# Four edits to the order of TensorE's work in a hybrid recurrent layer: the triangular inversion's two updates, half-block gemms, SSD's carried part, the output weights' splits

## The chip, the cores and the metric

One Trainium2 chip, one core, one launch. The metric is the device time of one execution in microseconds; lower is better. Engines are called as in the profile: PE is TensorE's matmuls, PEld its weight loads, DVE is VectorE, ACT is ScalarE, POOL is GpSimd, SP is the queue that issues the DMAs.

## The reference, cut to what matters

The layer takes 1024 prompt tokens and 8 x 8 sample tokens (1088 tokens of width 1024). It projects them, runs four recurrent mixers of width 256, and projects back:

```
z   = x @ w_in
A   = RG-LRU(conv(z_a)) * SiLU gate
B   = gated RMSNorm(SSD(conv(z_b)))          chunked scan
C   = RMSNorm(GatedDeltaNet(conv(z_c))) * SiLU gate
D   = GLU(S5(z_d)) * SiLU gate
out = concat(A, B, C, D) @ w_out
x   = LayerNorm(alpha * x + out)
```

Gated DeltaNet (GDN), per chunk and head, needs the inverse of a unit lower triangular matrix:

```
m     = where(strict, beta * (k k^T) * gamma, 0)
tmat  = inverse(eye + m)
value = tmat @ (beta * v);  kcum = tmat @ (beta * exp(decay) * k)
w     = value - kcum @ s
o     = qdec @ s + (q k^T * gamma) @ w
s     = chunk_decay * s + kdec^T @ w
```

SSD, per chunk and head:

```
y  = (C B^T * L * dt) @ x  +  (C * exp(acum)) @ h_prev  +  d * x
h  = chunk_decay * h + (exp(acum_last - acum) * dt * B)^T @ x
```

## The kernel before, in words

**Gemms.** Tokens are held transposed in SBUF as a rounded part and a rest (`xh`, `xl`), and so are the weights. A product of 128 output columns is `gemm_ch` (L237): it loads and splits the weights (`load_w`, L142: a DMA, an ACT copy into `wh`, a DVE subtraction into `wl`) and calls `gemm_block` (L227) for three blocks of tokens of 320, 384 and 384 columns. A block is 24 matmuls into one PSUM bank (lines L232, L233, L234), and then ACT or DVE takes the bank away. Twelve of these 18 products run in the part of the program that the change touches.

**Two streams.** From about 200 us on, the last line of the program, `run(merge((gdn(...), 130.0), (side(), 280.0)))`, walks two generators. Each `yield c` says how much work was issued since the last one, and `merge` (L112) goes on with the stream that is furthest behind its share. This sets the order in which instructions are emitted. The framework then orders each engine's instructions from it when the program is built, earlier emitted ones first where they are expected to be ready; an engine runs its list strictly in that fixed order. So between two matmuls of the inversion there stand a few matmuls of a gemm block that was emitted as a whole.

**The GDN stream** takes nine chunks (64 sample tokens, then 8 x 128 prompt tokens). While `tail` of a chunk runs (state update, output), `make` of the next one runs `prep` and `invert` (L834). `invert` doubles the size of the inverted blocks level by level, 3 levels for the sample chunk and 6 for each other, 51 in all. X and Y (the inverse and its transpose, four heads side by side) are kept in one PSUM bank `XY`, X in the first 256 columns and Y in the others. A level is:

- L861: T = A X on PE, into another bank; L863: DVE multiplies it by the level's mask into `t_`; L852 (`spread`): two DVE copies into `tb`
- L868: X += Y^T T on PE (reads `t_` and the copy `yb` of Y); L870: ACT copies X out
- L873: Y += T^T Y on PE (reads `tb` and Y); L876: two ACT copies into `yb`; L878: ACT copies Y out

A `yield 0.2` stands after X and another after Y. After the levels comes one correction step (E by L882 and L883, its DVE part L885 into `tb`, then L890 on PE).

**The side stream** (L1347) issues the gemms, RG-LRU, SSD (`chunk`, L1067) and then the out projection (`project`, L1395). SSD uses a pool of two PSUM banks (tag "b") in turn for `xt`, `gam`, `cb0`, `cb1`, `yd`, `yo0`, `yo1`, `st` and `yT`. C B^T is L1090; DVE makes M of it (L1093); M x is L1101 into the bank `yd`; the carried part C h is L1114 into the banks `yo0` and `yo1`; L1117 adds it.

**The out projection.** `woh` and `wol`, the split parts of w_out, take the SBUF space of `xh` and `xl`, so that no split can be written before the last gemm has read those. `w_half` (L1400) loads eight pieces of 128 x 512, one for each k; ACT writes `woh` (L1405), DVE `wol` (L1406). The loads go into the buffers of the gemms' weights (tags `wr` with 2 buffers, `wh` and `wl` with 4 each). Then for each of nine token chunks: load x (L138), gate v (L1422), split the eight pieces of the mixers' output for k = 0 to 3 and 4 to 7 (ACT L1428, DVE L1429, also in buffers of the tags `wh` and `wl`), and for each half of the columns 24 matmuls (L1439 to L1441), a residual add and statistics; the second half of w_out is split between the first chunk's own splits and its matmuls. Layer norm and the store follow.

Of the kernel before, what the change touches and what calls it, by code (L numbers as in the profile page):

```python
# [14 lines left out]
OP = mybir.AluOpType  # L15
# [4 lines left out]
P = 128  # L20
# [32 lines left out]
def hybrid_step(ctx, tc, I, O, dbg=None):  # L53
    nc = tc.nc
    mm = nc.tensor.matmul
# [171 lines left out]
    def gemm_block(w, a, b, evac):  # L227
        whi, wlo = w
        ps = gemm_bank()
        o = ps[:, :b - a]  # L230
        for k in range(8):
            mm(o, whi[k], xh[:, k, a:b], start=(k == 0), stop=False)  # L232
            mm(o, whi[k], xl[:, k, a:b], start=False, stop=False)  # L233
            mm(o, wlo[k], xh[:, k, a:b], start=False, stop=(k == 7))  # L234
        evac(a, b, o)

    def gemm_ch(c0, evac):  # L237
        w = load_w(w_tile(c0), P)
        for a, b in BLOCKS:
            gemm_block(w, a, b, evac)  # L240
            yield 3.7
# [525 lines left out]
    def gdn(wk, up, q, k, v, rk, rq):  # L767
# [66 lines left out]
        def invert(d):  # L834
# [23 lines left out]
            for l in range(3 if n == NS else 6):  # L858
# [8 lines left out]
                for h in range(4):  # L867
                    mm(pX[:n, h], idh[:n, :n] if Y is None else yb[:n, h, :n], t_[:n, h], start=False, stop=False, skip_group_check=True)  # L868
                X = pk(f16("X", "X", 256, 2))
                act(X[:n], pX[:n], AF.Copy)  # L870
                yield 0.2
                for h in range(4):
                    mm(pY[:n, h], tb[:n, h, :n], idp[:n] if Y is None else Y[:n, h], start=False, stop=h == 3, skip_group_check=True)  # L873
# [175 lines left out]
    def ssd(wk, up, x, BT, CT):  # L1049
# [17 lines left out]
        def chunk(ti):  # L1067
# [20 lines left out]
            for g in range(2):  # L1088
                sl = slice(g * 64, g * 64 + 64)
                mm(pcb[g][:n, :n], BT[sl, c], CT[sl, c], start=True, stop=True)  # L1090
            M = g2("M")
# [7 lines left out]
            py = bank("yd")  # L1099
# [5 lines left out]
            tt(y[:n], py[:n, :256], y[:n], OP.add)  # L1105
            if ti != 1:
# [3 lines left out]
                else:  # L1110
                    pyo = [bank("yo0"), bank("yo1")]
                    for g in range(2):
                        sl = slice(g * 64, g * 64 + 64)
                        mm(pyo[g][:, :P], CT[sl, c], Hs[sl].rearrange("p h d -> p (h d)"), start=True, stop=True)  # L1114
                    yof = lambda h: pyo[h // 2][:, 64 * (h % 2):64 + 64 * (h % 2)]
# [279 lines left out]
    def project():  # L1395
# [4 lines left out]
        def w_half(e):  # L1400
            for k_ in range(8):
# [6 lines left out]
        w_half(slice(0, 512))  # L1408
# [5 lines left out]
        for i in range(9):  # L1414
# [9 lines left out]
            for k0 in (0, 4):  # L1424
                h_, l_ = (wp.tile([P, 536], F32R, name=nm(t), tag=t)[:, :4 * n].rearrange("p (k n) -> p k n", k=4) for t in ("wh", "wl"))
# [121 lines left out]
```

## Time and profile before

| | |
|---|---|
| median of 3 runs | 619.89 us (618.18 to 621.85) |
| the profiled execution, its own time | 620.72 us |
| its span, first to last instruction | 619.0 us |
| granted TensorE clock, mean over the span | 0.988 |
| instructions | 11787 |
| DMA | 44.14 MB, mean 71 GB/s |

Times in the rows are microseconds from the start of the span. In a timeline row stand the start, the duration, engine, line, operation, the tiles written and read, the shape and how many equal instructions were merged; in brackets the idle time of the engine before it and what ended it. Matmuls are pipelined, and their ends are modelled: the distance from one start to the next is what a matmul takes of PE.

### The profile page before, as it was taken

What the parts mean: (1) busy time and instruction counts of PE and PEld (TensorE: products, weight loads), DVE (VectorE), ACT (ScalarE), POOL (GpSimd) and SP (SyncE); (2) the same over time, 40 slices, a digit from 0 to 9 for tenths busy, and PEclk for the clock granted to TensorE, in tenths of its full rate; (3) what the DMA queues carried; (4) which work ended last, traced back from release to release, by engine and by line L of the source; (5) the groups of instructions that cost most, each with busy time, mean ns of one, the idle gap of its engine ahead of it and who ended that gap; (6) DMA issues with size and microseconds to landing.
All of it is one profiled execution on the core that took longest, in us unless ns stands there. A gap on an engine that the chain in (4) does not pass through costs nothing.

```text
span 619.0 us, 11787 instructions
## 1 busy us (share of the span) xinstructions
PE 586.3 (95%) x4284; PEld 503.4 (81%) x4284; DVE 464.9 (75%) x1372; ACT 325.0 (53%) x877; POOL 62.7 (10%) x165
## 2 busy tenths in 40 slices
PE   5999899999999999999999999999999799999995
PEld 5999899999998776888887888787877557778883
DVE  6997989943768586699888867786775789866655
ACT  5545255345364457897665665766546657332210
POOL 8220100000100000211001000110010000110000
PEclk9999999999899999999999999999999999999998
DMA  8552212041310010010142100110033221121221
GB/s 301 171 169 63 77 65 78 16 131 73 119 40 19 19 44 29 17 35 19 39 143 80 43 5 23 37 43 10 2 125 110 77 94 53 40 101 69 102 103 68
DMA packets 24187, 44.14 MB, mean 71 GB/s; under 512 B 3201, under 2 KB 10433, under 8 KB 24129
## 3 DMA queue, kind: packets, MB, share of 16 engines
q1 hardware_dynamic: 24128, 43.38, 21.4%
q8 instruction: 34, 0.56, 0.4%
q14 instruction: 25, 0.20, 0.1%
HBM read 32.97 MB, written 10.41 MB: 70 GB/s over the span
## 4 chain that ended last, share of the span: by engine, by line
PE 65%; DVE 16%; ACT 8%; issue 6%; DMA 3%; POOL 2%; SPq 1%; DVEq 0%; ACTq 0%; POOLq 0%
PE pg L234 7%; PE pg L232 7%; PE pg L233 7%; PE pg L1441 5%; PE pg L1440 5%; PE pg L1439 5%; DVE acc L266 2%; ACT yb L876 2%; PE ssq L760 1%; DMA wr<-in_w_tiles_dram 1%; PE XY L868 1%; DVE cm L469 1%; PE pg L403 1%; DVE cm L468 1%; PE pg L405 1%
## 5 line engine op out<-in xcount | busy, mean ns | idle before, releaser
L232 PE MATMUL pg<-xh,wh 128*128 128x384 f32 (+1 forms) x432 | 149.1, 345 | 0.0
L234 PE MATMUL pg<-xh,wl 128*128 128x384 f32 (+1 forms) x432 | 147.7, 342 | 0.0
L233 PE MATMUL pg<-xl,wh 128*128 128x384 f32 (+1 forms) x432 | 147.1, 341 | 0.0
L234 PEld LDWEIGHTS pg<-xh,wl 128*128 128x128 f32 x432 | 82.0, 190 | 2.6 <-issue 1.2
L232 PEld LDWEIGHTS pg<-xh,wh 128*128 128x128 f32 x432 | 82.2, 190 | 2.2 <-issue 0.5
L233 PEld LDWEIGHTS pg<-xl,wh 128*128 128x128 f32 x432 | 82.2, 190 | 1.9 <-issue 1.2
L1439 PE MATMUL pg<-woh,wh 128*128 128x512 f32 (+1 forms) x144 | 58.2, 404 | 3.1 <-ACT wh L1428 3.1
L1440 PE MATMUL pg<-wol,wh 128*128 128x512 f32 (+1 forms) x144 | 58.5, 406 | 0.0
L1441 PE MATMUL pg<-woh,wl 128*128 128x512 f32 (+1 forms) x144 | 57.9, 402 | 0.1
L266 DVE SCALAR_TENSOR_TENSOR acc<-z,pcol,acc 128x1112 f32<-128x1112 f32 x36 | 49.4, 1371 | 1.9 <-ACT acc L264 1.5
L156 ACT ACTIVATE wh<-wr 128x512 fp32r<-128x512 f32 (+1 forms) x40 | 25.2, 632 | 32.8 <-PE pg L233 26.4
L876 ACT ACTIVATE yb<-XY 64x256 f16<-64x256 f32 x82 | 31.0, 378 | 15.6 <-PE XY L873 13.3
L1439 PEld LDWEIGHTS pg<-woh,wh 128*128 128x128 f32 (+1 forms) x144 | 26.4, 183 | 10.2 <-ACT wh L1428 3.5
L870 ACT ACTIVATE X<-XY 128x256 f16<-128x256 f32 (+1 forms) x51 | 19.5, 383 | 27.5 <-PE XY L868 27.2
L1441 PEld LDWEIGHTS pg<-woh,wl 128*128 128x128 f32 (+1 forms) x144 | 26.5, 184 | 7.7 <-DVE wl L1429 0.9
L1440 PEld LDWEIGHTS pg<-wol,wh 128*128 128x128 f32 (+1 forms) x144 | 26.5, 184 | 6.5 <-issue 0.4
L863 DVE TENSOR_TENSOR T<-T,lev 128x256 f16<-128x256 f32 (+1 forms) x51 | 21.4, 419 | 13.4 <-PE T L861 13.0
L244 ACT ACTIVATE z<-pg 128x384 f32<-128x384 f32 (+2 forms) x48 | 17.5, 396 | 25.1 <-PE pg L234 23.6
L157 DVE TENSOR_TENSOR wl<-wr,wh 128x512 fp32r<-128x512 f32 (+1 forms) x40 | 27.8, 697 | 2.2 <-ACT wh L156 1.8
L742 ACT ACTIVATE gam<-gam,nac 128x128 f32<-128x128 f32 (+1 forms) x72 | 21.0, 374 | 5.9 <-PE gam L739 5.9
L1442 DVE SCALAR_TENSOR_TENSOR y<-y,pg 128x512 f32<-128x512 f32 (+1 forms) x18 | 12.3, 682 | 15.0 <-PE pg L1441 14.9
L403 PE MATMUL pg<-wh,xh 128*128 128x268 f32 x72 | 20.7, 288 | 2.7 <-ACT bg L408 2.7
(443 smaller groups left out, 1331.7 us busy)
## 6 DMA issues: line engine op xcount, KB each, us to landing
wr<-in_w_tiles_dram SPq DMA_DIRECT2D x40, 256.0 KB, 2.8
x<-in_x_t_dram SPq DMA_DIRECT2D x8, 544.0 KB, 5.1
wo<-in_w_out_dram SPq DMA_DIRECT2D x16, 256.0 KB, 3.0
y<-in_x_dram SPq DMA_DIRECT2D x8, 512.0 KB, 3.3
out_y_dram<-y SPq DMA_DIRECT2D x7, 512.0 KB, 2.6
bgd<-bg SPq DMA_DIRECT2D x9, 128.0 KB, 1.8
dud<-us SPq DMA_DIRECT2D x2, 544.0 KB, 4.5
U<-dud SPq DMA_DIRECT2D x16, 68.0 KB, 2.7
```

The costliest lines, as they stand in the source:

```text
L156: act(hv_, wv, AF.Copy)
L157: lo_eng[0].tensor_tensor(lv, wv, hv_.bitcast(F32), OP.subtract)
L232: mm(o, whi[k], xh[:, k, a:b], start=(k == 0), stop=False)
L233: mm(o, whi[k], xl[:, k, a:b], start=False, stop=False)
L234: mm(o, wlo[k], xh[:, k, a:b], start=False, stop=(k == 7))
L266: stt(acc[:, :CL], s[:, j:j + CL], col(wkey, j * nt + i), acc[:, :CL], OP.mult, OP.add)
L403: mm(o, xh[:, k, c0:c0 + P], whi[k], start=(k == 0), stop=False)
L863: tt(t_[:n], pt[:n], lev[:n, l].unsqueeze(1).to_broadcast([n, 4, 64]), OP.mult)
L876: act(yb[s, :, s], pY[s], AF.Copy)
L1439: mm(ps[:n], mh[k_], woh[:, k_, e], start=(k_ == 0), stop=False)
L1440: mm(ps[:n], mh[k_], wol[:, k_, e], start=False, stop=False)
L1441: mm(ps[:n], ml[k_], woh[:, k_, e], start=False, stop=(k_ == 7))
```

## The change

In the inversion, Y's update is emitted ahead of X's, and X's update is ordered on PE behind the last matmul of Y's; one of a level's two yields goes. `gemm_block` becomes a generator that yields 1.85 after k = 3 and after its end, where `gemm_ch` yielded 3.7 after the block. In SSD the carried part's matmuls go into columns 128 to 255 of the banks `cb0` and `cb1`, right behind C B^T, and M x into columns 256 to 511 of `cb0`; the banks `yd`, `yo0` and `yo1` are no longer taken (the sample chunk keeps its own `yo`). In the out projection the first half of w_out is loaded and split in two parts of four k, each ahead of the first chunk's own splits for the same four k; the loads of `ln_g`, `ln_b` and the first x come before it. No arithmetic is added or left out.

```diff
@@ gemm_block, gemm_ch
             mm(o, wlo[k], xh[:, k, a:b], start=False, stop=(k == 7))
+            if k % 4 == 3 and k < 7:
+                yield 1.8500
         evac(a, b, o)
+        yield 1.8500
 
     def gemm_ch(c0, evac):
         w = load_w(w_tile(c0), P)
         for a, b in BLOCKS:
-            gemm_block(w, a, b, evac)
-            yield 3.7
+            yield from gemm_block(w, a, b, evac)
@@ invert
                 for h in range(4):
-                    mm(pX[:n, h], idh[:n, :n] if Y is None else yb[:n, h, :n], t_[:n, h], start=False, stop=False, skip_group_check=True)
+                    last = mm(pY[:n, h], tb[:n, h, :n], idp[:n] if Y is None else Y[:n, h], start=False, stop=h == 3, skip_group_check=True)
+                with tc.issue_after(last.ins):
+                    for h in range(4):
+                        mm(pX[:n, h], idh[:n, :n] if Y is None else yb[:n, h, :n], t_[:n, h], start=False, stop=False, skip_group_check=True)
                 X = pk(f16("X", "X", 256, 2))
                 act(X[:n], pX[:n], AF.Copy)
-                yield 0.2
-                for h in range(4):
-                    mm(pY[:n, h], tb[:n, h, :n], idp[:n] if Y is None else Y[:n, h], start=False, stop=h == 3, skip_group_check=True)
@@ ssd, chunk
                 mm(pcb[g][:n, :n], BT[sl, c], CT[sl, c], start=True, stop=True)
+            if ti > 1:
+                for g in range(2):
+                    sl = slice(g * 64, g * 64 + 64)
+                    mm(pcb[g][:, P:2 * P], CT[sl, c], Hs[sl].rearrange("p h d -> p (h d)"), start=True, stop=True)
...
-            py = bank("yd")
+            py = pcb[0][:, 2 * P:]
...
-            tt(y[:n], py[:n, :256], y[:n], OP.add)
+            tt(y[:n], py[:n], y[:n], OP.add)
...
-                    pyo = [bank("yo0"), bank("yo1")]
-                    for g in range(2):
-                        sl = slice(g * 64, g * 64 + 64)
-                        mm(pyo[g][:, :P], CT[sl, c], Hs[sl].rearrange("p h d -> p (h d)"), start=True, stop=True)
-                    yof = lambda h: pyo[h // 2][:, 64 * (h % 2):64 + 64 * (h % 2)]
+                    yof = lambda h: pcb[h // 2][:, P + 64 * (h % 2):P + 64 + 64 * (h % 2)]
@@ project
-        def w_half(e):
-            for k_ in range(8):
+        def w_half(e, ks=range(8)):
+            for k_ in ks:
...
-        w_half(slice(0, 512))
         lnp = []
...
             for k0 in (0, 4):
+                if i == 0:
+                    w_half(slice(0, 512), range(k0, k0 + 4))
```

## Rows read from the trace of the kernel before

**Rows 1.** The page's first part: busy time, share of the span, instructions.

```profile
PE 586.3 (95%) x4284; PEld 503.4 (81%) x4284; DVE 464.9 (75%) x1372; ACT 325.0 (53%) x877; POOL 62.7 (10%) x165
```

**Rows 2.** Busy time by stretch: us, engines, PE clock, DMA share, GB/s.

```profile
200.00:543.00 343.00, 329.54 (x2704) 266.75 (x2704) 263.86 (x734) 214.13 (x625) 31.68 (x62) 1.00 0.16 50
543.00:619.00 76.00, 67.70 (x291) 53.99 (x289) 45.43 (x114) 16.30 (x44) 5.16 (x8) 0.97 0.23 85
```

**Rows 3.** Timeline of PE, a level of the inversion and the T before it.

```profile
470.64 0.28 PE L861 MATMUL T<-X,ah 128*128 128x64 f16 x4
...
472.14 0.28 PE L868 MATMUL XY<-T,yb 128*128 128x64 f16 x4 [0.26 <-ACT Y L878]
472.25 0.42 PE L232 MATMUL pg<-xh,wh 128*128 128x384 f32 x1
472.51 0.34 PE L233 MATMUL pg<-xl,wh 128*128 128x384 f32 x1
472.69 0.34 PE L234 MATMUL pg<-xh,wl 128*128 128x384 f32 x1
472.89 0.28 PE L873 MATMUL XY<-Y,tb 128*128 128x64 f16 x4
473.00 0.28 PE L861 MATMUL T<-X,ah 128*128 128x64 f16 x4
...
474.50 0.28 PE L868 MATMUL XY<-T,yb 128*128 128x64 f16 x4 [0.26 <-ACT Y L878]
```

**Rows 4.** Timeline of ACT in the same level.

```profile
472.45 0.38 ACT L870 ACTIVATE X<-XY 128x256 f16<-128x256 f32 x1
473.26 0.78 ACT L876 ACTIVATE yb<-XY 64x256 f16<-64x256 f32 x2 [0.42 <-PE XY L873]
474.07 0.38 ACT L878 ACTIVATE Y<-XY 128x256 f16<-128x256 f32 x1
```

**Rows 5.** Timeline of DVE, mask and copies behind that first T.

```profile
470.96 0.42 DVE L863 TENSOR_TENSOR T<-T,lev 128x256 f16<-128x256 f32 x1 [1.83 <-PE T L861]
471.42 0.46 DVE L852 COPY tb<-T 64x256 f16<-64x256 f16 x2
```

**Rows 6.** Waits of PE, 200 to 543 us: us in total, times, longest.

```profile
PE XY L868 <- ACT Y L878: 3.3, 13, 0.4
PE XY L868 <- DVE T L863: 1.6, 2, 1.2
PE F L890 <- DVE tb L885: 1.0, 2, 0.6
```

**Rows 7.** Timeline of PE, a carried product between gemm matmuls.

```profile
378.24 0.30 PE L232 MATMUL pg<-xh,wh 128*128 128x320 f32 x1
378.47 0.48 PE L1114 MATMUL yo<-Hs,z 64*128 64x128 f32 x2
378.89 0.41 PE L233 MATMUL pg<-xl,wh 128*128 128x320 f32 x1
```

**Rows 8.** Timelines of PE, ACT, DVE and SP where the out projection begins.

```profile
494.36 0.50 PE L1439 MATMUL pg<-woh,wh 128*64 128x512 f32 x1 [3.13 <-ACT wh L1428]
...
498.27 0.39 PE L1439 MATMUL pg<-woh,wh 128*64 128x512 f32 x1
498.50 0.39 PE L1440 MATMUL pg<-wol,wh 128*64 128x512 f32 x1
...
491.41 2.75 ACT L1405 ACTIVATE woh<-wo 128x512 fp32r<-128x512 f32 x5
494.01 0.73 ACT L1428 ACTIVATE wh<-z 128x64 fp32r<-128x64 f32 x4
...
505.21 1.13 DVE L1406 TENSOR_TENSOR wol<-wo,woh 128x512 fp32r<-128x512 f32 x1 [0.19 <-ACT woh L1405]
...
483.24 18.97 SPq L1404 DMA_DIRECT2D wo<-in_w_out_dram  x10
```

**Rows 9.** Busy time in one microsecond of it; columns as in the second group.

```profile
496.00:497.00 1.00, 1.00 (x4) 0.57 (x3) 1.00 (x3) 1.00 (x6) 0.00 (x0) 0.50 0.88 264
```

## The prediction

> **What bounds the kernel now.** I read the page first. PE is busy for 95% of the span, DVE for 75%, ACT for 53% [rows 1]: PE is the bound, and 619 less 586 us of idle time is all that such a reading leaves. Then the stretches. The edits act from about 200 us, where the two streams start, to 543 us, where GDN ends; there PE is busy for 329.5 of 343 us, and the 76 us behind it are out projection alone [rows 2]. The order of two independent streams on a full engine changes nothing by itself, so each edit is to be costed by what it takes off PE in that stretch: idle time, and time that busy time hides.
>
> The timeline shows the hidden kind [rows 3]. Undisturbed gemm matmuls start 0.18 us apart (472.51 to 472.69). The first one behind four small matmuls of the inversion takes 0.26 (472.25 to 472.51). So each return to a gemm costs about 0.09 us, besides the small matmuls themselves (0.11 for four: 472.14 to 472.25).
>
> It also shows the level's chain. From one L868 to the next is 474.50 - 472.14 = 2.36 us. X's copy runs on ACT from 472.45 to 472.83 [rows 4], and L873 starts at 472.89 [rows 3]. Its `tb` is long there: copies of that kind end 471.88 - 470.64 = 1.24 us behind their T [rows 3, 5]. It waited for X's copy, though that reads other columns: X and Y lie in one PSUM bank. Then come two `yb` copies and Y's, 473.26 to 474.45 [rows 4], and again L868 follows 0.05 us behind the last reader of the bank, after 0.26 us of idle PE [rows 3].
>
> **The change, part by part.**
>
> *Inversion.* Its three times four matmuls a level stay. PE's visits stay too: before, X's update alone, then Y's with the next T; after, Y's with X's, then T alone. So no return to a gemm is saved. What changes is the waits. Before, Y's update waited for X's copy and the next X's update for Y's. After, both write the bank, then ACT reads it four times in a row: 0.31 us until X's copy, 0.38 for it, 0.78 and 0.38 for the others with some 0.03 between them, so Y's copy ends about 1.9 us behind X's update [rows 3, 4]. Beside that runs T: L861 could follow X's copy as L873 does now, 472.89 - 472.14 = 0.75 us behind X's update, and `tb` ends 1.24 behind that [rows 3, 5]: about 2.0. With 0.06 for the hop to PE and 0.11 for Y's four matmuls the cycle is some 2.2 us where it was 2.36. A shorter cycle is not PE's time as long as gemms fill it; the waits are. PE's waits for L868 are 3.3 + 1.6 us in 15 cases [rows 6]; the idle time is counted from a matmul's modelled end, which lies 0.34 - 0.18 = 0.16 us behind the next possible start [rows 3], so 15 x 0.16 = 2.4 more are hidden: 7.3 us in all, 0.14 for each of 51 levels. The added wait is L873's for `tb`. Behind it on PE's fixed list stand X's update, then gemm matmuls and T; for X's update wait ACT's X copy and so the next T. Before, X's copy came later than `tb` and covered that wait, so I bound it: none at all, if the list puts enough gemm matmuls ahead (gain 7.3); 0.15 a level by the nearest row, L890's wait for two DVE results of this kind, (1.0 + 2 x 0.16) over nine chunks [rows 6] (loss 0.3). I take 0.10, nearer to the row, since L852's copies take 0.23 each and L885's source is PSUM: 5.1 us for 51. **Gain 2.2 us.** The dropped yields (0.2 a level, 1.2 of a chunk's 10.5) let GDN run about a tenth further ahead of the side stream; cost nothing, since PE has gemms or out projection to fill with until the end; if that cover went, a level would show its 2.2 us bare.
>
> *Half blocks.* The same 24 matmuls and the same evacuation. Gemm matmuls already stand in short pieces between the visits, three in the rows shown [rows 3], so a yield after twelve adds no visit: 0. Bounds: 36 blocks with one more return of 0.09 each, +3.2; the same the other way, -3.2.
>
> *SSD.* Fourteen pairs of L1114 (seven chunks) go right behind L1090. A pair that stands alone costs 0.23 - 0.15 on the way in (378.24 to 378.47, where a 320 column matmul is 0.15 by its 320/384 of 0.18) and 0.09 on the way out, 0.17 us; its own matmuls take 0.42 either way [rows 7]. In the timeline three of the fourteen stand so, the first of them the row shown; a fourth has a gemm on one side, the others stand beside other small work. **Gain 3 x 0.17 + 0.09 = 0.6 us**; ends: all fourteen, 2.4, and none, 0, to which the rival of the shared bank adds a loss.
>
> *Out projection.* PE stands for 3.13 us until 494.36, because ACT made five `woh` pieces (2.75 us from 491.41) before the first chunk's own split for k = 2 [rows 8]. Behind the idle time the clock is granted at 0.50, the 1.2 GHz level [rows 9]: nine matmuls from 494.36 to 498.27 take 3.91 us, at 0.23 each (498.27 to 498.50) 2.1 [rows 8], 1.8 lost; 4.9 in all. After, only the fourth `woh` (a fifth of 2.75) stands ahead of k = 2 and 3, so PE goes on about 2 us earlier; then it meets k = 4, whose split stands behind four more `woh`, 2.2 us, against 6 x 0.23 = 1.4 of matmuls: 0.8 lost again. That leaves 1.2 of idle time and perhaps the clock's 1.8. But the second half of w_out does not come sooner: its DVE splits end at 506.3 [rows 8], held by loads whose issue waits for buffers until 502 [rows 8], and what is gained ahead of it is partly waited out there. The moved DMAs: `ln_g`, `ln_b` and x now go ahead of w_out's first loads on SP, and the first chunk's splits take one `wh` and one `wl` buffer ahead of the pieces k = 4 to 7; those loads have some 20 us until the last gemm frees `xh`, so cost nothing; uncovered, one load's issue waits longer, about a microsecond. **Gain 2 us**; ends 4.9 and -1.
>
> **Sum**: 2.2 + 0.6 + 2 = 4.8 us off the profiled execution's 620.72 (its span and 1.7 around it, which stay) is 615.9; the median shown, 619.89, is 0.83 below that execution, so I predict 619.89 - 4.8 = **615.1 us**.
>
> **The rivals.**
>
> *Slower: X's update pays for `tb`.* Before, X's update needed only `t_`; now it stands behind Y's, which needs two more copies, 0.46 us [rows 5]. Where the fixed list was made for an earlier `tb`, PE stops at L873 and everything behind stops with it. At 0.14 + 0.18 (one gemm matmul too few) = 0.32 us a level that is 16.3 us for 51, less 7.3 saved and 2.6 from the other parts: 6.4 slower, 626.3. It decides from (7.3 + 2.6)/51 = 0.19 us a level on. For it: DVE is the second fullest engine [rows 1]. Against it: the old chain had a wait of the same making and held it at 0.14.
>
> *The waits only move.* L873 takes over what L868 waited, the out projection waits at its second half for what it no longer waits at its first: 619 to 620. For it: the bank and the DVE remain as they are, and both gains are of waits. It includes that `issue_after` only orders the two updates and does not shorten the level.
>
> *SSD's shared bank.* By the mechanism that the timeline shows for X and Y, M (L1093) cannot read C B^T before the carried matmuls into the same bank are done: 14 x 0.21 = 2.9 us more in SSD's chain; shown in full it leaves a gain of 4.8 - 2.9 = 1.9, 618.0. Against it: SSD's chain is beside the gemms. The Trainium skill, PSUM — Partial Sum Buffer, section on bank collisions, says to guard PSUM by bank and quadrant rather than by address; the trace agrees (0.06 us between X's copy and L873), and by this rule the sharing edit costs rather than saves.
>
> *All of it.* No wait at L873, no idle time or half clock at the out projection: 7.3 + 0.6 + 4.9 = 12.8, 607.1.
>
> **How the numbers follow.** The measurement tells 0.5%, 3.1 us, from no change. Chances: forecast 0.45, all of it 0.12, waits only move 0.19, shared bank 0.07, slower 0.17. The first two are faster by over 0.5%: 0.57. The next two lie within it: 0.26. Slower 0.17. The range goes from below *all of it* (the half blocks' end on part of it), 605, to the near side of the slower case, 624, which leaves out some 0.2.
>
> **What would show it.** L873 directly followed by L868 and T alone; PE's waits named L873 from `tb`, under 6 us, in place of L868's from Y; X, `yb`, `yb`, Y in a row on ACT; L1114 behind L1090 with no rows of its own between gemms; L1439's wait for L1428 under 1.5 us; GDN ending well ahead of 543 us. Wrong would be waits at L873 over 0.2 us a level, PE idle in the middle of the span because GDN runs ahead, or the second half of w_out ending later than now.

## The result and the profile after

The kernel after takes 606.68 us (median; 604.04 to 610.73), the kernel before in the same comparison 622.20 (618.18 to 625.87). The ratio is 0.976, 95% interval 0.973 to 0.979: 15 us less, three times the 4.8 that were forecast. Runs more than 1.5% above their kernel's fastest are left out of all ratios; that takes out eight of the twelve runs of the inversion alone, one of six at weight 140 and two of the kernel before. The profiled execution took 608.82 us, its span 607.1, where before it was 620.72 and 619.0. Lines below L234 stand mostly two or three further down in the code, so L861 is now L863, L868 is L873 (X), L873 is L870 (Y), L1014 is L1016, L1439 is L1442.

The page's first part for the kernel after, then its busy time by stretch with the columns of [rows 2]; GDN's last output matmul (L991, last row) starts at 508.7 us, where before it started at 540.5.

```profile
PE 582.5 (96%) x4284; PEld 505.9 (83%) x4284; DVE 461.9 (76%) x1372; ACT 320.7 (53%) x877; POOL 57.1 (9%) x165
```

```profile
200.00:509.00 309.00, 303.05 (x2625) 251.16 (x2624) 246.87 (x688) 203.91 (x609) 26.60 (x67) 0.99 0.16 50
509.00:607.00 98.00, 90.67 (x390) 72.38 (x388) 62.44 (x165) 22.97 (x63) 6.46 (x10) 0.98 0.23 84
```

```profile
L991 PE MATMUL o<-W,Pm x72: 218/275/323, 240.3 to 508.7; 128*128 128x64 f32 x64, 64*64 64x64 f32 x8
```

Beside [rows 1] little has changed: PE has the same 4284 matmuls, is 3.8 us less busy, and 12 us of span are gone. Beside [rows 2] it stands idle 6.0 us up to GDN's end where it was 13.5. Over the whole span 8.1 of the 11.9 us that are gone were idle PE (619.0 - 586.3 against 607.1 - 582.5), and 3.8 were time for which PE counted as busy.

A level of the inversion, by the timelines of PE, ACT and DVE of the kernel after (to set beside [rows 3 to 5]):

```profile
477.57 0.29 PE L870 MATMUL XY<-Y,tb 128*128 128x64 f16 x4
477.69 0.28 PE L873 MATMUL XY<-T,yb 128*128 128x64 f16 x4
477.81 0.42 PE L234 MATMUL pg<-xh,wl 128*128 128x384 f32 x1
478.07 0.34 PE L232 MATMUL pg<-xh,wh 128*128 128x384 f32 x1
478.25 0.33 PE L233 MATMUL pg<-xl,wh 128*128 128x384 f32 x1
478.50 0.28 PE L863 MATMUL T<-X,ah 128*128 128x64 f16 x4
...
479.79 0.29 PE L870 MATMUL XY<-Y,tb 128*128 128x64 f16 x4
```

```profile
478.07 0.38 ACT L875 ACTIVATE X<-XY 128x256 f16<-128x256 f32 x1 [0.44 <-PE XY L873]
478.35 0.77 ACT L878 ACTIVATE yb<-XY 64x256 f16<-64x256 f32 x2
479.14 0.38 ACT L880 ACTIVATE Y<-XY 128x256 f16<-128x256 f32 x1
```

```profile
478.82 0.42 DVE L865 TENSOR_TENSOR T<-T,lev 128x256 f16<-128x256 f32 x1
479.28 0.46 DVE L854 COPY tb<-T 64x256 f16<-64x256 f16 x2
```

Y's update is followed by X's, X, `yb`, `yb`, Y go in a row on ACT, T stands alone, and `tb` is ready (479.74) just before Y's update needs it. The level takes 479.79 - 477.57 = 2.22 us.

PE's waits from 200 to 545 us in the kernel after, beside [rows 6] (us in total, times, longest):

```profile
PE XY L870 <- DVE tb L854: 2.8, 6, 0.9
PE J L906 <- DVE x L902: 0.8, 1, 0.8
PE oT L1016 <- DVE o L1013: 0.5, 1, 0.5
PE yT L1146 <- DVE y L1142: 0.4, 2, 0.2
```

The waits for ACT's Y and the out projection's 3.1 us for `wh` are gone, and a wait for `tb` has come, 2.8 us where X's update waited 3.3 + 1.6.

SSD, timeline of PE, beside [rows 7]; below it, from the rows on tile M, what DVE idled for before it made M (us, times):

```profile
442.97 0.48 PE L1092 MATMUL cb<-z,z 64*128 64x128 f32 x2
443.29 0.38 PE L1096 MATMUL cb<-Hs,z 64*128 64x128 f32 x2
443.48 0.48 PE L1092 MATMUL cb<-z,z 64*128 64x128 f32 x2
443.90 0.29 PE L863 MATMUL T<-X,ah 128*128 128x64 f16 x4
```

```profile
  PE cb L1096: 1.5, 2
```

The six matmuls from 442.97 on, C B^T of two chunks and one carried pair, take 443.90 - 442.97 = 0.93 us, where three pairs at the 0.42 of [rows 7] are 1.26. M now does wait for the carried matmuls, as the shared bank's rival had it, but for 1.5 us in all, and off PE's path.

The out projection's start, timeline of PE, and a microsecond behind it, beside [rows 8, 9]:

```profile
490.69 0.38 PE L1016 MATMUL oT<-idf,o 128*128 128x128 f32 x2
491.83 0.65 PE L906 MATMUL J<-x,A 64*64 64x64 f32 x8 [0.76 <-DVE x L902]
492.46 0.44 PE L1442 MATMUL pg<-woh,wh 128*64 128x512 f32 x1
492.95 0.80 PE L909 MATMUL J<-Yf,x 64*64 64x64 f32 x8
```

```profile
494.00:495.00 1.00, 1.00 (x3) 0.45 (x2) 1.00 (x3) 0.98 (x4) 0.00 (x0) 0.50 0.71 188
```

There GDN's last chunk stands among the first output matmuls, 3.1 us of idle time have become 0.8, and the clock still falls to 0.50 (the 1.2 GHz level), from 493.4 to 500.2 us, twice as long as before (494.6 to 498.0).

Where the 12 us of span lie, by busy time from GDN's first matmul to the last gemm and from the first output chunk to the last output matmul; two rows of the kernel before, then two of after:

```profile
198.20:486.00 287.80, 279.18 (x2380) 231.66 (x2380) 217.18 (x592) 180.66 (x524) 28.17 (x56) 1.00 0.14 46
507.00:611.20 104.20, 102.42 (x543) 80.60 (x541) 72.25 (x210) 33.49 (x94) 7.10 (x11) 1.00 0.21 75
```

```profile
201.20:490.50 289.30, 284.15 (x2533) 238.29 (x2533) 229.58 (x648) 190.00 (x572) 26.29 (x59) 1.00 0.14 44
510.70:599.30 88.60, 88.60 (x383) 71.24 (x381) 56.36 (x152) 22.55 (x62) 5.54 (x9) 1.00 0.24 87
```

Some 153 of GDN's matmuls have moved from the out projection into the gemms. The later stretch is 15.6 us shorter, and the earlier one takes them in for 1.5 us more. That asks for an explanation: moved work should cost as much in its new place.

### The profile page after: what moved, and what is told of

The parts are those of the page before. It is cut to its first block, busy times and chain, and to the rows that moved or that the text cites. A ratio compares the mean times of both kernels' runs of the same rounds, so it can differ in the third digit from the quotient of the medians.

```text
span 607.1 us, 11704 instructions
## 1 busy us (share of the span) xinstructions
PE 582.5 (96%) x4284; PEld 505.9 (83%) x4284; DVE 461.9 (76%) x1372; ACT 320.7 (53%) x877; POOL 57.1 (9%) x165
## 4 chain that ended last, share of the span: by engine, by line
PE 72%; DVE 15%; ACT 5%; issue 3%; DMA 3%; POOL 1%; SPq 1%; DVEq 0%; ACTq 0%; POOLq 0%
PE pg L233 8%; PE pg L232 8%; PE pg L234 8%; PE pg L1443 6%; PE pg L1442 6%; PE pg L1444 6%; PE kq L825 2%; PE ssq L762 1%; DMA wr<-in_w_tiles_dram 1%; DVE acc L268 1%; PE cb L1107 1%; PE pg L405 1%; DVE cm L471 1%; PE pg L406 1%; PE pg L407 1%
## 5 line engine op out<-in xcount | busy, mean ns | idle before, releaser
L234 PE MATMUL pg<-xh,wl 128*128 128x384 f32 (+1 forms) x432 | 148.0, 343 | 0.0
L234 PEld LDWEIGHTS pg<-xh,wl 128*128 128x128 f32 x432 | 82.8, 192 | 1.7 <-issue 0.8
L1442 PE MATMUL pg<-woh,wh 128*128 128x512 f32 (+1 forms) x144 | 57.6, 401 | 0.0
L1442 PEld LDWEIGHTS pg<-woh,wh 128*128 128x128 f32 (+1 forms) x144 | 26.5, 184 | 7.4 <-ACT woh L1407 0.4
L865 DVE TENSOR_TENSOR T<-T,lev 128x256 f16<-128x256 f32 (+1 forms) x51 | 21.5, 421 | 11.4 <-PE T L863 10.2
L1458 ACT ACTIVATE y<-y,nb,rs 128x1024 f32<-128x1024 f32 (+1 forms) x8 | 10.0, 1244 | 23.9 <-DVE nb L1457 12.8
## 6 DMA issues: line engine op xcount, KB each, us to landing
x<-in_x_t_dram SPq DMA_DIRECT2D x8, 544.0 KB, 4.8
dud<-us SPq DMA_DIRECT2D x2, 544.0 KB, 4.6
```

Of the source, the lines that this page charges most:

```text
L865: tt(t_[:n], pt[:n], lev[:n, l].unsqueeze(1).to_broadcast([n, 4, 64]), OP.mult)
L1442: mm(ps[:n], mh[k_], woh[:, k_, e], start=(k_ == 0), stop=False)
```

## The experiments

All ratios are against the kernel before on the same chip, with 95% intervals. Three more numbers help to read them. **Span at full clock**: within each kernel the spans of its runs lie on a line against the mean granted clock, for the kernel before 612.2 us + 0.54 us for each 0.001 below 1 (103 runs on five chips, clocks 0.974 to 0.992, residual 0.4 us); the table gives where each kernel's line meets full clock. Slopes of kernels with few runs are loose (0.29 to 0.65): with the slope of before for all, the entries move by up to 2.3 us (the kernel after to 596.8), that without `issue_after` by 3.7. **Visits**: over all rows of PE from the first L861 on, the runs of small matmuls between two large ones (gemm or out projection). **Waits**: the same rows, start to start, outside half clock, all that lies above a matmul's usual distance (the quarter point of its kind) where it is over 0.15 us; another choice of the usual distance moves the entries by up to 3 us, that of SSD alone by 5. The last column is the start of GDN's last output matmul in the profile.

| kernel | ratio | full clock, us | visits | waits, us | GDN ends |
|---|---|---|---|---|---|
| before | 1 | 612.2 | 187 | 31.2 | 540.5 |
| after | 0.976 [0.973, 0.979] | 599.1 | 157 | 21.0 | 508.7 |
| inversion alone | 0.998 [0.992, 1.003] | 606.7 | 162 | 24.9 | 534.5 |
| half blocks alone | 1.002 [0.999, 1.005] | 611.9 | 198 | 31.0 | 542.2 |
| SSD alone | 0.998 [0.995, 1.001] | 611.2 | 186 | 33.2 | 540.0 |
| out projection alone | 0.997 [0.995, 1.000] | 612.5 | 186 | 31.0 | 540.3 |
| without inversion | 0.993 [0.990, 0.997] | 610.3 | 198 | 33.0 | 542.7 |
| without half blocks | 0.990 [0.985, 0.995] | 602.4 | 154 | 27.9 | 519.7 |
| without SSD | 0.990 [0.984, 0.995] | 605.5 | 161 | 26.3 | 514.8 |
| without out projection | 0.975 [0.970, 0.980] | 599.2 | 155 | 22.7 | 506.9 |
| new order, old pace | 0.999 [0.997, 1.001] | 609.0 | 181 | 32.0 | 544.0 |
| old order, new pace | 0.989 [0.987, 0.992] | 607.8 | 173 | 27.0 | 515.1 |
| the same, weight 126 | 0.989 [0.986, 0.992] | 607.5 | 181 | 29.3 | 522.5 |
| the same, weight 134 | 0.988 [0.985, 0.991] | 607.2 | 174 | 31.5 | 496.9 |
| after, weight 126 | 0.979 [0.976, 0.982] | 603.2 | 154 | 24.2 | 513.8 |
| after, weight 134 | 0.987 [0.984, 0.990] | 604.8 | 153 | 30.2 | 504.6 |
| after, weight 140 | 0.987 [0.982, 0.992] | 602.7 | 154 | 25.6 | 503.1 |
| after, weight 150 | 0.997 [0.994, 1.000] | 609.9 | 162 | 29.3 | 502.4 |
| before, weight 147 | 1.002 [0.999, 1.004] | 613.8 | 180 | 32.4 | 518.6 |
| after, no `issue_after` | 0.976 [0.973, 0.978] | 600.5 | 157 | 22.5 | 505.5 |

### Each part alone

*The inversion alone* (order and dropped yield on the kernel before):

```diff
                 for h in range(4):
-                    mm(pX[:n, h], ...)
+                    last = mm(pY[:n, h], ...)
+                with tc.issue_after(last.ins):
+                    for h in range(4):
+                        mm(pX[:n, h], ...)
                 X = pk(f16("X", "X", 256, 2))
                 act(X[:n], pX[:n], AF.Copy)
-                yield 0.2
-                for h in range(4):
-                    mm(pY[:n, h], ...)
```

> Only the inversion's edit (Y's update first, X's behind it, one yield of a level dropped). Theory 'GDN runs ahead': the dropped yields let GDN end well before 540 us (under 525) and most of out projection runs undisturbed, so most of the change's 2.4% is here: 7 to 12 us faster. Rival 'waits alone': PE's waits at the update fall by what the prediction took, 2 to 5 us faster, and GDN's end does not matter. Rival 'sum of small parts': under 4 us here.

Measured: median 625.92 against 621.79, ratio 0.998 [0.992, 1.003]. Its runs spread from 616.5 us at a mean clock of 0.985 to 635.9 at 0.950, far more than any other kernel's. On its line to full clock it is 5.5 us shorter than before, with 25 visits fewer; by its runs as they are, the gain cannot be told from none. By the line the clock takes it: the mean over its runs is 0.967, where the kernel before has 0.985. Its profile (635.85 us, clock 0.950) shows two stretches of 17 us at the 1.2 GHz level among the gemms, and 13.7 us more from 512.8 on; columns as in [rows 2]:

```profile
359.00:376.00 17.00, 17.00 (x88) 14.15 (x87) 6.58 (x20) 6.29 (x24) 0.55 (x1) 0.50 0.05 16
437.00:455.00 18.00, 18.00 (x93) 13.93 (x91) 6.58 (x21) 6.25 (x23) 0.00 (x0) 0.53 0.05 15
```

Just ahead of the first two, PE waited at the transposes L1014 and L1144, at most 1.2 us from one start to the next (356.9 and 435.1). The profiles without the inversion, without half blocks, and of the new order at the old pace (below) show the same behind such a wait of 1.2 to 1.7 us: some 10 us at 0.50 from 417.6, 362.3 and 416.3. In the kernels before and after the clock falls between 200 and 595 us at the out projection's start only. Each of these is one execution.

*Half blocks alone*:

```diff
             mm(o, wlo[k], xh[:, k, a:b], start=False, stop=(k == 7))
+            if k % 4 == 3 and k < 7:
+                yield 1.8500
         evac(a, b, o)
+        yield 1.8500
...
-            gemm_block(w, a, b, evac)
-            yield 3.7
+            yield from gemm_block(w, a, b, evac)
```

> Only the gemms' half blocks. The prediction and 'GDN runs ahead': within 2 us of before, since no matmul and no visit is added. Rival 'finer order': the small matmuls gather in fewer visits, 3 to 6 us faster.

Measured: 1.002 [0.999, 1.005]. Eleven visits more; at the forecast's 0.09 us for a return that is 1.0 us; the median is 0.7 above before, less than the interval tells.

*SSD alone*:

```diff
+            if ti > 1:
+                for g in range(2):
+                    sl = slice(g * 64, g * 64 + 64)
+                    mm(pcb[g][:, P:2 * P], CT[sl, c], Hs[sl].rearrange("p h d -> p (h d)"), start=True, stop=True)
...
-            py = bank("yd")
+            py = pcb[0][:, 2 * P:]
...
-                    pyo = [bank("yo0"), bank("yo1")]
...
-                        mm(pyo[g][:, :P], CT[sl, c], Hs[sl].rearrange("p h d -> p (h d)"), start=True, stop=True)
```

> Only SSD's carried part in the banks of C B^T. The prediction: 0.6 us faster, at most 2.4; the shared bank's rival: up to 2.9 us slower. A third reading: fewer banks taken in turn let SSD's other matmuls gather, 3 us or more faster.

Measured: 0.998 [0.995, 1.001], no change that can be told. The 64 matmuls of C B^T and of the carried part take, start to start, 9.6 us in place of 11.6, in 23 unbroken rows in place of 32.

*The out projection alone*:

```diff
-        w_half(slice(0, 512))
...
+                if i == 0:
+                    w_half(slice(0, 512), range(k0, k0 + 4))
```

> Only the out projection's splits in turn. The prediction: 2 us faster, the wait of 3.1 us for the first chunk's own split falls under 1.5. 'GDN runs ahead': 1 to 3 us. Rival 'the waits only move': within 1 us, the time is waited out at the second half of w_out.

Measured: 619.97 against 621.79, 0.997 [0.995, 1.000]; by its line to full clock nothing. The 3.1 us for which L1439 waited for L1428 [rows 8] are 0.8 in PE's waits between 200 and 545 us (there L1440 and L1429), and two lines have come beside it:

```profile
PE pg L1441 <- DVE wol L1406: 1.0, 2, 0.7
...
PE pg L1440 <- ACT wh L1429: 0.8, 1, 0.8
PE pg L1440 <- ACT woh L1405: 0.5, 2, 0.3
```

Added up, the four parts alone give 1 - 0.998 + 1 - 1.002 + 1 - 0.998 + 1 - 0.997 = 0.5%, a fifth of what they give together. On the line to full clock they give 5.5 + 0.3 + 1.0 - 0.3 = 6.5 of 13.1 us, a half: part of what is missing is the clock that the inversion alone loses.

### Each part left out

*Without the inversion*: the kernel after with the old order of the updates and the old yields.

```diff
                 for h in range(4):
-                    last = mm(pY[:n, h], ...)
-                with tc.issue_after(last.ins):
-                    for h in range(4):
-                        mm(pX[:n, h], ...)
+                    mm(pX[:n, h], ...)
                 X = pk(f16("X", "X", 256, 2))
                 act(X[:n], pX[:n], AF.Copy)
+                yield 0.2
+                for h in range(4):
+                    mm(pY[:n, h], ...)
```

> The whole change without the inversion's edit (the old order of X and Y, both yields). Theory 'GDN runs ahead' (the inversion's edit carries the change, the others help it): the gain falls to 1 to 4 us against before, and GDN again ends after 535 us with out projection's matmuls cut by it. Rival 'the parts only meet together' (no part alone gave over 0.3%, so any one missing loses most): as well under 4 us. Rival 'half blocks carry it': still over 8 us faster.

Measured: 0.993 [0.990, 0.997]. The other three give 0.7%, 4 us, and GDN ends at 542.7 us again; the inversion's edit makes 1.7% on top of them and nothing measurable alone.

*Without half blocks*:

```diff
-            if k % 4 == 3 and k < 7:
-                yield 1.8500
         evac(a, b, o)
-        yield 1.8500
...
-            yield from gemm_block(w, a, b, evac)
+            gemm_block(w, a, b, evac)
+            yield 3.7
```

> The whole change without the half blocks. 'GDN runs ahead': GDN still ends before 520 us and most of the gain stays, 9 to 13 us faster than before. Rival 'the half blocks place the other stream's steps between the gemm's matmuls': half of the gain or more goes, under 7 us faster, and stretches at half clock come back in the middle of the span.

*Without SSD*:

```diff
-            if ti > 1:
-                for g in range(2):
-                    sl = slice(g * 64, g * 64 + 64)
-                    mm(pcb[g][:, P:2 * P], CT[sl, c], Hs[sl].rearrange("p h d -> p (h d)"), start=True, stop=True)
...
-            py = pcb[0][:, 2 * P:]
+            py = bank("yd")
...
+                    pyo = [bank("yo0"), bank("yo1")]
```

> The whole change without SSD's shared banks. By the part alone (under 1.5 us): 11 to 14 us faster than before. Rival 'SSD's waits meet GDN's once GDN runs ahead' (the waits of the transposes L1014 and L1144 after that are longest with the inversion's edit alone): 4 to 9 us are lost, and stretches at half clock come back.

*Without the out projection's edit*:

```diff
+        w_half(slice(0, 512))
...
-                if i == 0:
-                    w_half(slice(0, 512), range(k0, k0 + 4))
```

> The whole change without the out projection's splits in turn. By the part alone (about 2 us, half of it fewer microseconds at half clock): 11 to 13 us faster than before. Rival 'GDN has ended by then, so nothing covers the splits': 4 to 7 us are lost at the out projection's start.

Measured: 0.990 without half blocks, 0.990 without SSD, 0.975 without the out projection's edit. So without half blocks or SSD, each nothing alone, 1.4% of the time comes back, nearer to the rival theories than to the small losses of the first ones; without the out projection's edit nothing does. These shares hold for the weight 130 alone. The whole change loses 1.1% by a step to 134 (below), so how much of each 1.4% is the edit's own, and how much is that the two lists fall otherwise without it, no run tells; by the intervals each share is known to some 0.6%. For half blocks some of it is clock: the mean over the runs without them is 0.977, in the kernel after 0.984, and at full clock the loss is 3.3 us. In the kernel without the out projection's edit the timeline of PE shows why its wait does not come back:

```profile
489.05 0.45 PE L1441 MATMUL pg<-woh,wh 128*64 128x512 f32 x1 [0.47 <-ACT woh L1407]
489.79 0.65 PE L906 MATMUL J<-x,A 64*64 64x64 f32 x8 [0.30 <-DVE x L902]
490.90 0.90 PE L909 MATMUL J<-Yf,x 64*64 64x64 f32 x8 [0.47 <-ACT x L907]
```

The last chunk of GDN, further ahead now, fills the time in which ACT splits w_out. The shares of the four leave-outs add up to 1.7 + 1.4 + 1.4 - 0.1 = 4.4%, nearly twice the whole: they do not add.

### Order and pace

The inversion's edit does two things: it turns the order of the updates, and it drops a yield, which lets GDN be emitted further ahead (a chunk costs 9.3 in place of 10.5). Two kernels take one without the other, both with the three other edits. The old order keeps two yields of 0.1 where the new one has one of 0.2, so the number of places at which the other stream can come in goes with the order; no run parts the two.

*New order, old pace*:

```diff
-                yield 0.2
+                yield 0.4
```

> The whole change with the new order of Y and X, but a level issues 0.4 again (its one yield is 0.4 instead of 0.2), so that GDN is emitted at the pace of before. Theory 'pace' (what counts is that GDN runs ahead): most of the inversion's share is lost, 2 to 5 us faster than before in all, as without the inversion's edit, and GDN ends after 535 us. Theory 'order' (what counts is the level's shorter cycle and X, Y in one visit): 10 to 14 us faster than before all the same. If both count: 6 to 9 us.

*Old order, new pace*:

```diff
                 for h in range(4):
                     mm(pX[:n, h], ...)
                 X = pk(f16("X", "X", 256, 2))
                 act(X[:n], pX[:n], AF.Copy)
+                yield 0.1
                 for h in range(4):
                     mm(pY[:n, h], ...)
...
-                yield 0.2
+                yield 0.1
```

> The whole change with the old order of X and Y and both yields, but each 0.1, so that a level issues 0.2 as after the change. Theory 'pace': 10 to 14 us faster than before, as with the whole change, and GDN ends before 520 us. Theory 'order': 3 to 6 us faster, as without the inversion's edit. If both count: 6 to 9 us.

Measured: 0.999 and 0.989. With neither 0.993, with both 0.976. At the old pace the new order costs 0.5%; at the new pace it brings 1.3%. At full clock: 610.3 with neither, 609.0 and 607.8 with one, 599.1 with both. For the old order at the new pace the case that both count came (6.6 us); the new order at the old pace gained less than any of the three had it. There the rival of the prediction by which the waits only move came: in the profile's rows of waits X's and Y's updates wait 3.5 us in place of 4.7, but by the table all waits together are 32.0 us in place of 33.0.

*A still quicker pace*:

```diff
-    run(merge((gdn(wk, up, q, k, v, *rn), 130.0), (side(), 280.0)))
+    run(merge((gdn(wk, up, q, k, v, *rn), 150.0), (side(), 280.0)))
```

> The whole change with GDN's share in the last merge at 150 instead of 130, so GDN runs further ahead still. Theory 'pace' taken on: GDN ends before 490 us, and 1 to 4 us more are gained than by the change. Rival 'the change's pace is enough': out projection runs undisturbed already, so within 2 us of the change, or slower by idle PE and half clock where GDN stands alone at each level.

Measured: 0.997 [0.994, 1.000]. GDN ends earlier than in the kernel after (502.4 us), the out projection is as free of it (its later stretch takes 88.2 us, as the 88.6 above), and nearly all of the gain is gone. So an early end of GDN is not the cause by itself.

*Without `issue_after`*:

```diff
-                with tc.issue_after(last.ins):
-                    for h in range(4):
-                        mm(pX[:n, h], ...)
+                for h in range(4):
+                    mm(pX[:n, h], ...)
```

> The whole change without the pin that holds X's update behind Y's on TensorE; the emission order stays Y, X. If the pin matters, X's update, whose mask product is ready before the two copies, goes ahead again, X and Y take two visits, and 2 to 5 us of the change's gain are lost. If not, within 2 us of the change.

Measured: 0.976 [0.973, 0.978], as the kernel after. The order in which the updates are emitted is enough.

### Is it the weight 130?

The streams' weight moves the point at which one list meets the other. Neighbouring weights, first for the whole change:

```diff
-    run(merge((gdn(wk, up, q, k, v, *rn), 130.0), (side(), 280.0)))
+    run(merge((gdn(wk, up, q, k, v, *rn), 126.0), (side(), 280.0)))
```

> The whole change with 126 in place of 130 as the weight of the GDN stream in the last merge, so GDN 3% further behind the side stream than in the change (606.7 us). Smooth effect of pace: 604 to 609 us, GDN ends within 8 us of the change's 508.7 and the waits at the transposes stay between 2 and 4 us. Alignment of the two lists: the gain is not kept, 610 us or more for this or the next weight, with 4 us or more of waits at the transposes L1014 and L1144.

The same with 134 and with 140:

> The whole change with weight 134, GDN 3% further ahead. Smooth effect of pace: 604 to 609 us, GDN ends at 500 to 509 us. Alignment: at least one of the weights 126 and 134 is 4 us or more slower than the change, whichever way GDN's end moves.

> The whole change with weight 140, half way to the 150 that measured 620.7 us. Smooth effect of pace: half way between the two, 610 to 617 us. Alignment: anywhere between 606 and 622 us, and not in the order of the weights.

Measured: 609.56, 614.03 and 614.72 us against 622.46. The first is within 3 us of the kernel after, the second 7 us slower, the third no slower than the second, and 150 another 6. A smooth effect of the pace would have kept 134 within 609 us: that theory falls. The waits name where the weights differ. PE's waits from 200 to 545 us at weight 134, the first lines and those of the transposes:

```profile
PE XY L870 <- DVE tb L854: 5.0, 7, 1.8
PE oT L1016 <- DVE o L1013: 1.6, 3, 0.7
PE pg L1444 <- DVE wl L1432: 1.2, 1, 1.2
PE yT L1146 <- DVE y L1142: 0.9, 2, 0.5
...
PE yT L1146 <- ACT gam L744: 0.7, 1, 0.7
PE oT L1016 <- DVE yss L1139: 0.6, 1, 0.6
```

Y's update and the transposes wait 5.0 + 1.6 + 0.9 + 0.7 + 0.6 = 8.8 us; in the kernel after 2.8 + 0.5 + 0.4 = 3.7.

*The kernel before with weight 147*, about the ratio of the streams that the dropped yields give:

```diff
-    run(merge((gdn(wk, up, q, k, v, *rn), 130.0), (side(), 280.0)))
+    run(merge((gdn(wk, up, q, k, v, *rn), 147.0), (side(), 280.0)))
```

> The kernel before with weight 147 in place of 130: its old order and its yields, at about the ratio of the streams that the change's dropped yields give. If the pace alone brings the out projection that GDN does not cut: GDN ends before 520 us (540.5 before) and the kernel is 3 to 6 us faster than before. If the pace needs the new order: GDN ends earlier too, but the waits at X's update grow from 10 us on and the time stays within 2 us of before.

Measured: 1.002 [0.999, 1.004]. Its two stretches, as above:

```profile
195.90:499.70 303.80, 292.50 (x2542) 240.99 (x2541) 231.12 (x642) 192.62 (x566) 25.48 (x59) 1.00 0.14 44
521.10:611.20 90.10, 89.75 (x388) 72.20 (x386) 56.81 (x155) 22.44 (x62) 5.56 (x9) 1.00 0.24 85
```

Here the out projection is freed too: 90.1 us in place of 104.2. But the gemms' stretch, which takes in the same matmuls, grows by 303.8 - 287.8 = 16 us. In this kernel moved work costs as much in its new place. So in the kernel after, the stretch that grew by only 1.5 us has shed some 14 us: that is where the gain lies. The weight moves GDN against the side stream only. The dropped yields also move `make` against `tail` in the merge of a chunk (L1041, weights 9.0 and 3.5); no run changed that alone, and none had weight 147 beside the other edits.

*The old order at the new pace*, at the weights 126 and 134 (the edit of the old order above, with these weights):

```diff
-    run(merge((gdn(wk, up, q, k, v, *rn), 130.0), (side(), 280.0)))
+    run(merge((gdn(wk, up, q, k, v, *rn), 134.0), (side(), 280.0)))
```

> The old order of the two updates with the new pace and the other three edits, weight 126. If the new order itself is worth the waits at X's update (7 to 10 us where the new order has 4 to 7 at Y's) and returns no visits, it lies 2 to 6 us above the change at the same weight: 612 to 616 us. If the gain at 130 was only how the lists fall, the two orders scatter over the same band: 606 to 612 us here or with 134.

> As before with weight 134. Order's own share: 2 to 6 us above the 614.0 of the new order, 616 to 620 us. Only how the lists fall: no higher than 614 us in one of the two runs.

Measured: 615.36 and 614.57 us; with 130 it was 615.50. The old order does not care for these three weights: 0.989, 0.989, 0.988. At 126 the time is in the range of an order with a share of its own; at 134 neither of the two forecasts held. PE's waits from 200 to 545 us at weight 126 begin so:

```profile
PE XY L870 <- ACT Y L880: 3.0, 12, 0.4
PE J L906 <- DVE x L902: 2.1, 2, 1.1
PE oT L1016 <- DVE o L1013: 1.7, 3, 0.8
```

It is X's update that waits for ACT's Y, a little every time, as in the kernel before. The new order gives 0.979, 0.976, 0.987 at the same three weights: better by 1.1%, 1.3% and 0.1%, each to some 0.4%.

**The account**, by the ratios to four digits, means over the weights 126, 130 and 134, in us of 622.2. Three other edits, old order and old pace: 1 - 0.9933, 4.2 us. The new pace, old order: 0.9933 - 0.9889, 2.7. The new order at the new pace: 0.9889 - 0.9806, 5.2. What the weight 130 has over the mean of the three: 0.9806 - 0.9759, 2.9. Together 15.0. The line to full clock gives 1.9, 2.8, 5.1 and 3.3 of 13.1, and with the slope of before for all 2.3, 3.7, 5.0 and 4.4 of 15.4. The intervals of the single steps are some 2 us wide to each side, and the first step was measured at the weight 130 only.

By what PE does, the same 13.1, to the 2 us that both readings leave open: the kernel after has 30 visits fewer than before, at 0.09 us for each return 2.7 us, and 31.2 - 21.0 = 10.2 us less of waits, together 12.9. The waits at X's and Y's updates fell from 10.6 to 4.2 us, at the transposes (L1014, L1144) from 4.8 to 2.3, at the out projection from 3.5 to none; other kinds rose and fell, by 2 us in sum upwards. What a return costs is taken from the one level of [rows 3], so the 2.7 us are an estimate. None of the variants is faster than the kernel after by more than the intervals.

## Why the prediction was right or wrong

**The bound.** Right: the gain is time taken off a full PE in the stretch of the two streams, waits and returns. Busy time hid a part of it, 3.8 of the 11.9 us of span; 8.1 were idle.

**The inversion's waits.** Right in mechanism: the waits for ACT's Y are gone, Y's update waits for `tb`, X's and Y's copies stand in a row, the level takes 2.22 us (forecast 2.2). The sizes were off. The old waits were taken at 7.3 us from the wait rows and 0.16 us hidden in each; start to start they are 10.6. The new ones were taken at 0.10 a level, 5.1 us; they are 2.8 + 6 x 0.16 = 3.8 by the same reading, 0.07 a level, 4.2 start to start. So this term is 6.4 in place of 2.2, in the whole change; with the new order at the old pace the updates wait less too, and the time does not fall. The slower rival, 0.32 us a level, did not come.

**"No return to a gemm is saved."** Right by the form of a level, wrong in the rows. Visits with a matmul of T, X, Y or E in them fell from 107 to 94 (of 188 and 158, the first one counted too). In the kernel before, the last Y of each of the nine chunks goes with E; after, E stands alone in four, so the levels' ends save nothing. The fall comes with the new order, at the old pace too (108 to 95 with the three other edits): T, and X with Y, more often fall beside other small work. No run took apart why.

**The dropped yields, "cost nothing".** This is the step that failed most: a term put at nothing. With the yields dropped, the whole change is at 0.976; with the sum of the yields as before, at 0.999, which is 14 us, both at the weight 130. The covering work was named rightly (PE has gemms or out projection until the end), and the kernel before with weight 147 shows that moving GDN ahead of the side stream by itself gives nothing. But the yields are not a matter of the end alone. They decide beside what the small matmuls stand: with the three other edits in, visits without the inversion are 91 at the old order and pace, 94 with the new order alone, 71 with the new pace alone, 68 with both. The pace is worth 2.7 us with the old order, and without it the new order's gain isn't there at all (0.999 against 0.993 with neither).

**Half blocks, 0 with bounds of 3.2 to both sides.** Right alone: eleven more visits, about 1 us. Left out of the whole change they cost 1.4%, 9 us, outside the bounds (3.3 at full clock); how much of that is theirs and not the lists' alignment at 130 is not shown.

**SSD, 0.6 us with ends 0 and 2.4.** Alone 0.998, within the interval of both. The step that said "its own matmuls take 0.42 either way" was wrong: in a row with C B^T six take 0.93. The unbroken rows of these matmuls fell from 32 to 17 in the kernel after, and its share there, 1.4%, is above the upper end, with the same reserve as for half blocks. The rival of the shared bank had beside it the Trainium skill, PSUM — Partial Sum Buffer, section on bank collisions, which says to guard PSUM by bank and quadrant rather than by address. The trace agrees that the reader waits for the bank's other writer (M for L1096, 1.5 us), but DVE idled 4.2 us for C B^T before, so no cost shows there.

**Out projection, 2 us.** About right alone (0.997; 1.7 us), nothing in the whole change, where GDN's last chunk covers the wait: the dropped yields remove what this term counted. One sign of being wrong came: the last split of w_out's second half ends at 509.35 + 0.68 = 510.0 us, where it was 506.3.

**The sum.** Four terms from one trace were added as if each kept its price beside the others. The runs show parts that give 0.5% alone (half of the whole at full clock), 2.4% together and 4.4% by leave-outs at the weight 130, and a new order whose share is -0.5%, 0.1%, 1.1% or 1.3% depending on pace and weight. The range reached to 605 and so held the result, by the case *all of it* at 607.1, which had a chance of 0.12; but that case is not what happened, since it counted 4.9 us at the out projection and none from pace. That the median lies within half a microsecond of it is luck. The signs named for the forecast (Y's update followed by X's, waits for `tb` under 6 us, GDN's early end, under 1.5 us at L1439) all came; they told the form of the change and not its size.

**What stays open.** Why 130 falls well for the new order, and 134 no better than the old one, is described by the waits and not derived: two fixed lists meet at other places, and nothing in the profile of before tells which places. The new order's waits are for DVE, few and long (7, up to 1.8 us, at weight 134), the old one's for ACT, many and short (12, up to 0.4, at 126); that would let the new order hang more on what DVE has in hand at the moment, but no run changed DVE's work to test it. Open too are the inner merge of a chunk, the number of yields, and how far the clock's falls behind the transposes' waits set the order of the kernels.

## What to carry to other kernels

When two independent instruction streams are merged into one fixed list on a full engine, an edit that changes how fast one of them is emitted is an edit to the whole list: give it a price and a width of its own, however little it computes. Measure such a change at neighbouring weights before believing either its gain or its absence, and its parts too; here the old order held within 1 us over three weights, the new one moved by 7. And count visits of small matmuls among large ones, start to start, in addition to the profile's idle time: of the 12 us of span gained in the profiled executions 8 show as idle PE (619.0 - 586.3 against 607.1 - 582.5).

## What the runs showed of the hardware that was not expected

The spread of one kernel's runs goes with the clock: for the kernel before, 0.001 of mean granted clock goes with 0.54 us of span over 103 runs, with a residual of 0.4 us. That line helps to tell kernels apart that lie within a few us, but it leaves out what a kernel loses because the clock falls in it: the inversion alone is 5.5 us shorter on the line, and its median over all twelve runs is 4.1 us longer. In its profile PE was held at the 1.2 GHz level for 17.1 us twice, behind waits of no more than 1.2 us from start to start.

Matmuls that contract 64 rows, on the lower and upper half of the partitions in turn, went at 0.155 us each in a row of six (442.97 to 443.90; the single distances go from 0.07 to 0.21) and at 0.21 in the pair of [rows 7]; of SSD's 64 such matmuls the next one started within 0.15 us at 28 in the kernel after, at 11 before. The Trainium skill, TensorEngine Tiling (Array Packing), key properties, says that different tiles of the array can load weights and multiply in parallel. The trace fits that in part only, since the pair of [rows 7], on both halves too, shows no overlap; no run here isolates it.
